# Split weights kept from quarters 1 to 3 for the dilation-4 query projection of quarter 4

## The chip, the core and the metric

The program runs on one core of a Trainium2 chip. Its time is the device time of one execution in microseconds, the median over runs. The engines are PE (matmul; PEld is its weight load), DVE (VectorE), ACT (ScalarE), POOL (GpSimd) and SP, which issues every transfer of this kernel in the order of its own instruction list: a transfer that has to wait holds back all that stand behind it. Sixteen DMA engines carry out what SP issues.

## The reference

A trunk of two layers on 2048 tokens of width 1024, in float32: a gated MLP with a causal spatial mixing inside chunks of 128, then one layer of sliding-window attention with three dilations (1, 4, 16) that share one K/V. The change is in the projection of the second layer:

```python
h = rms_norm(x, norm_g) * (1 + scale) + shift
qz = h @ w_in                      # 1024 -> 3 x 1024 (q of dilations 1, 4, 16) + 1024 (gate z)
q = rms_norm(q, q_norm_g) * (HEAD_DIM ** -0.5)
o, lse = dilated_group_attn(q[:, :, hs], kb, vb, slopes[hs], window, d)   # for each dilation
```

## The kernel before, in words

The 2048 tokens are worked off in four quarters of 512 (`for Q in range(NQ)`); the text counts them 1 to 4, the code 0 to 3. In each quarter `layer_A` does the first layer, then `proj_B` does the projections of the second: blocks 2 and 1 of K/V, `q_block(2)` (dilation 16), `kv_block(0)`, `q_block(1)` (dilation 4), `q_block(0)` (dilation 1) and `z_block`. Local attention of a quarter runs beside the next quarter's first layer. The dilation-16 attention needs all queries of that dilation, so it starts in quarter 4 only, as `wide_attention`, and is dealt out between the matmuls of `kv_block(0)`, `q_block(1)` and `q_block(0)` of that quarter, at a rate set by `rate` and `tick`.

A matmul in full precision is made of three in a faster format: a weight is split into a high part `hi` (a copy in float32r by ACT, line 252) and a low part `lo` (the difference, by DVE, line 253), `split`. `mm3` then does hi x hi, lo x hi and hi x lo. A q or z block (`dense_s`) takes seven products in place of eight, in the manner of Strassen's method: the weights of a product are one quadrant of the matrix ("11", "21", "22") or one of four sums of quadrants made once and stored (t1 to t4, in `wt`). The products run in the order 11, t2, 21, t3, t1, t4, 22. Each takes four k rows; a k row is a tile of 128 x 512, 256 KB as loaded and 512 KB when split, and feeds six matmuls. A product takes 24 of them.

`wunits` brings a k row: SP loads `raw` (pool `rp`, 6 buffers), ACT and DVE split it into `w` (pool `wp`, 8 buffers, so two products). So a raw load waits until the split six k rows earlier has been read, and a split waits until the matmuls eight k rows earlier are through. Every k row is loaded and split again in each of the four quarters.

The dilation-16 attention works on units of one block and four heads. For each unit SP loads the queries `qt` (`ap_`, 2 buffers), DVE copies their scale columns (`rt`, line 1309), PE transposes (`pq`), ACT makes `qT`, PE makes the scores (`ps`, line 1344), DVE adds the bias and finds the maxima (lines 1353 to 1357, into `pr` or `b_s`, then `stat`), ACT takes the exponential (line 1363), PE transposes (`pp`, line 1405), ACT or DVE copies to `pT`, PE multiplies with V (`po`, line 1423), and SP stores the output `ot` to `od`. A `qt` load waits for the transposes of the unit two before it.

The instruction order on each engine is set when the program is built: a scheduler places each instruction by its own estimate of when it can start. An engine then runs its list in that order.

In names of the program, `q31` is quarter 4 (index 3), dilation 4 (group 1); `raw_q31t` and `w_q31t` are a k row of a sum t1 to t4, `raw_q` and `w_q` one of a quadrant. `pd_q31a` and `pd_q31b` are the accumulators of that block.

Of the kernel before, what the change touches and what calls it, by code (L numbers as in the profile page):

```python
# [12 lines left out]
F32 = mybir.dt.float32  # L13
F32R = mybir.dt.float32r
# [4 lines left out]
P = 128  # L19
# [3 lines left out]
NQ = 4  # L23
# [11 lines left out]
def trunk(ctx, tc, out, x, c, a_ada_w, a_ada_b, a_norm_g, a_w_in, a_sgu_g, a_w_spatial,  # L35
          a_b_spatial, a_w_out, kv_ada_w, kv_ada_b, kv_norm_g, w_kv, k_norm_g, b_ada_w,
          b_ada_b, b_norm_g, b_w_in, b_q_norm_g, b_w_out, dbg=None):
    nc = tc.nc
# [26 lines left out]
    gd = dp.tile([2, D], F32, name="gd")  # L65
    wod = dp.tile([2, KT, P, 2, 512], F32, name="wod")
    hd = dp.tile([2, P, KT, 256], F32, name="hd")
    wtd = dp.tile([2, 7, 4, P, 2, 512], F32, name="wtd")
    wt = [[dp.tile([512, 512], F32, name=f"wt{b}_{i}") for i in range(4)] for b in range(6)]

# [184 lines left out]
    def wunits(w, k0, n0, nm, nk=KT, ordered=False):  # L255
        us = []
        for kk in range(nk):
            u = wp.tile([P, 2, 512], F32R, tag="w", name=f"w_{nm}{kk}")
            raw = rp.tile([P, 512], F32, tag="raw", name=f"raw_{nm}{kk}")
            ld = nc.sync.dma_start(raw, w[(k0 + kk) * P:(k0 + kk + 1) * P, n0:n0 + 512])  # L260
            last_ld[0] = ld
            if ordered:
                tc.keep_in_program_order(ld)
            split(u[:, 0, :], u[:, 1, :], raw)
            us.append(u)
        return us

    last_mm, last_ld = [None], [None]
# [274 lines left out]
    def sum_tile(nm):  # L543
        return tp.tile([P, 520], F32, tag="st", name=f"st_{nm}")

    def dense_s(ops, b, nm, evac):


        x, y = ([pst(f"pd_{nm}{c}{i}", "d") for i in range(2)] for c in "ab")
        if flip[0]:  # L550
            x, y = y, x
        flip[0] = not flip[0]
        w, n0 = block_of(b)
        src = {"11": (w, 0, n0), "21": (w, 4, n0), "22": (w, 4, n0 + 512)}
        src.update({f"t{i + 1}": (wt[b][i], 0, 0) for i in range(4)})

        def product(pts, a, w, first):
            us = wunits(*src[w], f"{nm}{w}_", 4)
            store_late(5)
            hh, hl = ops[a]  # L560
            for k in range(4):
                for i in range(2):
                    sl = slice(i * P, (i + 1) * P)
                    mm3(pts[i], hh[:, k, sl], hl[:, k, sl], us[k], first and k == 0, k == 3, True)
                tick(0.2857)
            job = jobs.pop(0) if jobs else None
            if job:
                with tc.issue_after(last_ld[0].ins):
                    job()

        def tmp(n):
            return [sum_tile(f"{nm}{n}{i}") for i in range(2)]

        def add(o, p, q):
            for i in range(2):
                nc.vector.tensor_tensor(o[i][:, 0:512], p[i], q[i][:, 0:512], ALU.add)

        product(x, "11", "11", True)
        u2 = tmp("u")
        for i in range(2):  # L580
            nc.scalar.activation(u2[i][:, 0:512], x[i], AF.Copy)
        product(y, "s2", "t2", True)
        add(u2, y, u2)
        product(x, "12", "21", False)
        for i in range(2):
            evac(i, x[i], 0)
        product(y, "s3", "t3", True)
        u3 = tmp("v")
        add(u3, y, u2)
        product(x, "s1", "t1", True)  # L590
        add(u3, x, u3)
        for i in range(2):
            evac(i + 2, u3[i], 1)
        product(y, "22", "t4", False)
        c21 = tmp("w")
        add(c21, y, u2)
        for i in range(2):
            evac(i + 2, c21[i], 0)
        product(x, "s4", "22", False)
        add(u2, x, u2)  # L600
        for i in range(2):
            evac(i, u2[i], 1)
# [544 lines left out]
    def proj_B(Q, hk, hb, keep, rest, ahead, ready):  # L1147
        def rows(t):
            return slice((Q * TPQ + t) * P, (Q * TPQ + t + 1) * P)

        def kvs(t, g0, n, part):

            return kvd[rows(t), g0:g0 + n // 2, :].rearrange(
                "p g (h two d) -> p g h two d", h=2, two=2)[:, :, :, part, :]

        def ev0(t, pt):
            held = Q == NQ - 1
            kt = head_norm_store(pt, 4, f"k0{Q}_{t}", held)[:, 0:512].rearrange("p (g h d) -> p g h d", g=2, h=2)

            def store():  # L1160
                for g in range(2):
                    nc.sync.dma_start(kvs(t, g, 2, 0)[:, 0], kt[:, g])
            if held:
                stores.append([4, store])
            else:
                store()

        def ev1(t, pt):
            kt = head_norm_store(pt, 2, f"k1{Q}_{t}")
            nc.scalar.activation(kt[:, 256:512], pt[:, 256:512], AF.Copy)  # L1170
            kt = kt.rearrange("p (g h d) -> p g h d", g=2, h=2)
            nc.sync.dma_start(kvs(t, 2, 2, 0)[:, 0], kt[:, 0])
            nc.sync.dma_start(kvs(t, 0, 2, 1)[:, 0], kt[:, 1])

        def ev2(t, pt):
            vt = evt(f"v2{Q}_{t}")
            nc.scalar.activation(vt, pt, AF.Copy)
            vt = vt.rearrange("p (g h d) -> p g h d", g=2, h=2)
            for g in range(2):
                nc.sync.dma_start(kvs(t, 1 + g, 2, 1)[:, 0], vt[:, g])  # L1180

        def kv_block(n, early=None, ready=None):
            dense([hk], w_kv, n * 512, f"kv{Q}{n}", (ev0, ev1, ev2)[n], early, ready)

        def q_block(g):
            def ev(t, src, n):
                if t < 2 and n == 0:
                    c_ = sum_tile(f"qc{g}{Q}{t}")
                    nc.scalar.activation(c_[:, 0:512], src, AF.Copy)
                    src = c_  # L1190
                nm = f"q{g}{n}{Q}_{t}"
                sq = evt(f"hs_{nm}")
                nc.scalar.activation(sq, src[:, 0:512], AF.Square)
                s4 = sp.tile([P, 16], F32, tag="sq", name=f"s4_{nm}")
                nc.vector.tensor_reduce(s4[:, 0:4], sq.rearrange("p (h d) -> p h d", d=P), AX.X, ALU.add)  # L1195
                nc.gpsimd.tensor_scalar(s4[:, 4:8], s4[:, 0:4], 1.0 / P, EPS, ALU.mult, ALU.add)  # L1196
                nc.gpsimd.tensor_tensor(src[:, 516:520], s4[:, 4:8], mhalf[:, 0:4], ALU.pow)
                nc.gpsimd.tensor_tensor(s4[:, 4:8], s4[:, 4:8], src[:, 516:520], ALU.mult)
                nc.gpsimd.tensor_tensor(src[:, 512:516], s4[:, 4:8],
                                        slopes[:, g * 8 + n * 4:g * 8 + n * 4 + 4], ALU.mult)  # L1200
                stores.append([4 if Q == NQ - 1 and g == 2 else 0,
                               lambda: nc.sync.dma_start(qd[g][rows(t), n, :], src)])
            dense_s(hb, g, f"q{Q}{g}", ev)

        def z_block(_):
            def ev(t, src, n):
                held = Q == NQ - 1 and (t, n) not in ((0, 0), (1, 0))
                zt = src[:, 0:512] if held else evt(f"zb{n}{Q}_{t}")
                nc.scalar.activation(zt, src[:, 0:512], AF.Silu)
                put = lambda: nc.sync.dma_start(zd[rows(t), n * 512:(n + 1) * 512], zt)  # L1210
                if Q == NQ - 1:
                    stores.append([-100 if held else 3, put])
                else:
                    put()
            dense_s(hb, 3, f"z{Q}b", ev)

        ops = make_ops(hb, keep, f"b{Q}")
        rate[0] = 1.7
        kv_block(2, {(0, 2): lambda: (rest(), fillers.insert(0, ops))}, ready)
        kv_block(1)  # L1220
        for _ in ops:
            pass
        if ops in fillers:
            fillers.remove(ops)
        while 2 not in combined:
            fill(1)
        q_block(2)
        if Q == NQ - 1:
            fillers.append(wide_attention())
            rate[0] = 9.2  # L1230
        kv_block(0)
        if Q < NQ - 1:
            drain()
            ahead()
        if Q == NQ - 1:
            for n in range(2):
                jobs.extend([None] * 2 + [lambda n=n: load_wo(0, 2 * n), None, None, lambda n=n: load_wo(0, 2 * n + 1), None])
            jobs.extend([None] * 4 + [lambda: (load_wo(1, 0), load_wo(1, 1)), lambda: load_wo(1, 2),
                                      lambda: load_wo(1, 3)])
        q_block(1)  # L1240
        q_block(0)
        if Q == NQ - 1:
            ahead()
        z_block(0)
        store_late(0)

# [436 lines left out]
```

## Time and profile before

| | |
|---|---|
| median of 3 runs | 2929.49 us (2927.91 to 2931.87) |
| the profiled execution | 2928.77 us, of it 2927.1 us span from the first to the last instruction |
| granted TensorE clock | 0.999 |
| `q_block(1)` of quarters 1, 2, 3 | 524 to 562, 1152 to 1190, 1794 to 1832 us |
| `q_block(1)` of quarter 4 | 2448 to 2541 us |

The stretches of the last two rows are read from the starts and ends of the matmuls on `pd_q01` to `pd_q31`. In quarters 1 to 3 the block's 168 matmuls run back to back, in quarter 4 they share PE with the attention, so the block lasts longer. All times in the text count from the start of the span. An engine's idle time matters only where PE has to wait for it.

### The profile page before, as it was taken

How to read it: one execution, taken by the hardware profiler on the slowest of the kernel's cores; microseconds unless marked ns; L12 is line 12 of the kernel's file. 1: busy time of each engine (PE TensorE's matmuls, PEld its weight loads, DVE VectorE, ACT ScalarE, POOL GpSimd, SP SyncE). 2: the span in 40 equal slices, each digit the busy share in tenths (PEclk: the TensorE clock that was granted, in tenths of full speed). 3: DMA queues.
4: the chain of work that ended last, by engine and by line, in shares of the span. 5: the costliest groups of instructions: out<-in, count | busy, mean ns of one | idle time of the engine just before them, and what ended most of it. 6: DMA issues, size and time to landing. Idle time of an engine off the chain costs nothing.

```text
span 2927.1 us, 45613 instructions
## 1 busy us (share of the span) xinstructions
PE 2881.6 (98%) x14608; PEld 2417.7 (83%) x14608; DVE 2161.1 (74%) x4070; ACT 1640.4 (56%) x3378; POOL 718.5 (25%) x1011
## 2 busy tenths in 40 slices
PE   7999999999999999999999999999999999999999
PEld 4788778888888878888888888888888888888887
DVE  6777676687777886887667776877768776878782
ACT  4323345767676355776555365774646367876441
POOL 1047102330000412501233213501414211222312
PEclk9999999999999999999999999999999999999999
DMA  8899976796888976787545976885337967789653
GB/s 280 264 298 341 322 246 191 241 302 213 275 292 307 343 250 213 253 298 245 169 121 191 344 226 213 284 269 168 107 103 250 329 200 240 249 272 336 220 172 112
DMA packets 393812, 713.54 MB, mean 244 GB/s; under 512 B 41722, under 2 KB 141276, under 8 KB 393572
## 3 DMA queue, kind: packets, MB, share of 16 engines
q1 hardware_dynamic: 393572, 710.63, 73.0%
q8 instruction: 116, 1.90, 0.3%
q14 instruction: 124, 1.02, 0.1%
HBM read 552.53 MB, written 157.95 MB: 243 GB/s over the span
## 4 chain that ended last, share of the span: by engine, by line
PE 80%; DMA 9%; DVE 5%; issue 3%; POOL 1%; ACT 1%; SPq 1%; POOLq 0%; ACTq 0%; DVEq 0%
PE pd_kv L281 8%; PE po L1423 4%; PE pd_u L323 3%; PE pd_u L325 3%; PE pd_z L325 3%; PE pd_z L323 3%; PE pd_u L324 3%; PE pd_z L324 3%; PE pd_o L281 2%; PE pm L1011 1%; PE pd_o3a L281 1%; DMA raw_u<-in_a_w_in_dram 1%; PE pd_o1a L281 1%; PE pd_v3b L281 1%; PE pd_v3a L281 1%
## 5 line engine op out<-in xcount | busy, mean ns | idle before, releaser
L281 PE MATMUL pd_kv<-w_kv,hkh 128*128 128x512 f32 x672 | 208.7, 391 | 1.4 <-DVE w_kv L253 1.3
L323 PE MATMUL pd_u<-hAh,w_u 128*128 128x512 f32 x512 | 207.0, 404 | 0.0
L323 PE MATMUL pd_z<-hAh,w_z 128*128 128x512 f32 x512 | 204.1, 399 | 0.0
L325 PE MATMUL pd_u<-hAh,w_u 128*128 128x512 f32 x512 | 200.5, 392 | 0.0
L325 PE MATMUL pd_z<-hAh,w_z 128*128 128x512 f32 x512 | 200.2, 391 | 0.0
L324 PE MATMUL pd_u<-hAl,w_u 128*128 128x512 f32 x512 | 199.7, 390 | 0.0
L324 PE MATMUL pd_z<-hAl,w_z 128*128 128x512 f32 x512 | 199.5, 390 | 0.0
L252 ACT ACTIVATE w_z<-raw_z 128x512 fp32r<-128x512 f32 x128 | 79.9, 631 | 142.0 <-PE pd_z L325 56.6
L252 ACT ACTIVATE w_u<-raw_u 128x512 fp32r<-128x512 f32 x128 | 79.5, 631 | 142.4 <-DMA raw_u<-in_a_w_in_dram 77.2
L1423 PEld LDWEIGHTS po<-kv,pT 128*128 128x128 f32 x1200 | 147.7, 191 | 11.8 <-ACT pT L1269 2.4
L1423 PE MATMUL po<-kv,pT 128*128 128x128 f32 x1200 | 150.8, 275 | 3.2 <-ACT pT L1269 1.6
L281 PEld LDWEIGHTS pd_kv<-w_kv,hkh 128*128 128x128 f32 x672 | 125.4, 188 | 28.5 <-DVE w_kv L253 2.5
L253 DVE TENSOR_TENSOR w_z<-raw_z,w_z 128x512 fp32r<-128x512 f32 x128 | 103.1, 817 | 53.5 <-ACT w_z L252 53.2
L1371 POOL TENSOR_TENSOR dg<-pr,ident 128x256 f32<-128x256 f32 x38 | 30.7, 808 | 434.6 <-DVE stat L1418 226.6
L281 PE MATMUL pd_kv<-w_kv,hkl 128*128 128x512 f32 x336 | 130.7, 390 | 0.0
L1363 ACT ACTIVATE pr<-pr,stat,rt 128x256 f32<-128x256 f32 (+1 forms) x192 | 104.3, 547 | 29.8 <-DVE stat L1357 16.1
L253 DVE TENSOR_TENSOR w_u<-raw_u,w_u 128x512 fp32r<-128x512 f32 x128 | 94.2, 747 | 35.2 <-ACT w_u L252 34.6
L252 ACT ACTIVATE w_q<-raw_q 128x512 fp32r<-128x512 f32 x144 | 89.0, 628 | 49.2 <-PE pd_kv L281 11.5
L253 DVE TENSOR_TENSOR w_q<-raw_q,w_q 128x512 fp32r<-128x512 f32 x144 | 95.8, 688 | 25.0 <-ACT w_q L252 22.8
L1196 POOL TENSOR_SCALAR s_q<-s_q 128x4 f32<-128x4 f32 x96 | 26.9, 280 | 353.7 <-DVE s_q L1195 275.8
L325 PEld LDWEIGHTS pd_u<-hAh,w_u 128*128 128x128 f32 x512 | 96.1, 188 | 21.4 <-DVE w_u L253 0.4
L325 PEld LDWEIGHTS pd_z<-hAh,w_z 128*128 128x128 f32 x512 | 96.1, 188 | 20.7
(906 smaller groups left out, 8511.7 us busy)
## 6 DMA issues: line engine op xcount, KB each, us to landing
raw_q<-in_b_w_in_dram SPq DMA_DIRECT2D x144, 256.0 KB, 3.2
w_o<-wtd SPq DMA_DIRECT2D x72, 512.0 KB, 4.7
raw_u<-in_a_w_in_dram SPq DMA_DIRECT2D x128, 256.0 KB, 4.3
raw_z<-in_a_w_in_dram SPq DMA_DIRECT2D x128, 256.0 KB, 3.7
wtd<-cs SPq DMA_DIRECT2D x56, 512.0 KB, 2.9
qt<-qd SPq DMA_DIRECT2D x96, 260.0 KB, 4.1
raw_v<-in_a_w_in_dram SPq DMA_DIRECT2D x96, 256.0 KB, 4.1
od<-ot SPq DMA_DIRECT2D x96, 256.0 KB, 3.0
```

Source lines behind the costliest of these rows:

```text
L252: nc.scalar.activation(hi, src, AF.Copy)
L253: nc.vector.tensor_tensor(lo, src, hi.bitcast(F32), ALU.subtract)
L281: last_mm[0] = nc.tensor.matmul(pt, a, u[:, w, :], start=f, stop=e, skip_group_check=more)
L323: nc.tensor.matmul(pts[i], wh, hh[:, k, :], start=k == 0, stop=False)
L324: nc.tensor.matmul(pts[i], wh, hl[:, k, :], start=False, stop=False)
L325: nc.tensor.matmul(pts[i], wl, hh[:, k, :], start=False, stop=k == KT - 1)
L1011: nc.tensor.matmul(pm[:, t * P:(t + 1) * P], m[e // 8][:, t, (e % 8) * P:(e % 8 + 1) * P], wst[:, e // 2, :], start=True, stop=True)
L1196: nc.gpsimd.tensor_scalar(s4[:, 4:8], s4[:, 0:4], 1.0 / P, EPS, ALU.mult, ALU.add)
L1363: nc.scalar.activation(pr[:, i, :], pr[:, i, :], AF.Exp, bias=mneg[:, i:i + 1], scale=u["rt"][:, h:h + 1], accum_out=lsum[:, i:i + 1])
L1371: nc.gpsimd.tensor_tensor(dg, prev, ident.unsqueeze(1).broadcast_to([P, hp, P]), ALU.mult)
L1423: nc.tensor.matmul(po[:, h * P:(h + 1) * P], u["pT"][h // hp][:, h % hp, j, :], u["kv"][:, j, kh, 1, :], start=j == 0, stop=j == nk - 1)
```

## The change

A new tensor in HBM, `qsd`, holds split k rows. In quarter 1 each of the seven products of `q_block(1)` stores its split k row 1, in quarter 2 its k row 2, in quarter 3 its k row 3: seven stores of 512 KB in each of three quarters. They are issued in the next product, after its weight loads (`saves`). In quarter 4 the block loads k rows 1, 2 and 3 of every product split, straight into `w` (21 loads of 512 KB in place of 21 of 256 KB), and splits only k row 0. `dense_s` of the other blocks is as before, apart from issuing what is left in `saves`.

```diff
@@ -65,6 +65,7 @@
     gd = dp.tile([2, D], F32, name="gd")
     wod = dp.tile([2, KT, P, 2, 512], F32, name="wod")
     hd = dp.tile([2, P, KT, 256], F32, name="hd")
+    qsd = dp.tile([2, 7, 4, P, 2, 512], F32, name="qsd")
     wtd = dp.tile([2, 7, 4, P, 2, 512], F32, name="wtd")
     wt = [[dp.tile([512, 512], F32, name=f"wt{b}_{i}") for i in range(4)] for b in range(6)]
 
@@ -543,7 +544,9 @@
     def sum_tile(nm):
         return tp.tile([P, 520], F32, tag="st", name=f"st_{nm}")
 
-    def dense_s(ops, b, nm, evac):
+    saves = []
+
+    def dense_s(ops, b, nm, evac, keep=(), kept=()):
 
 
         x, y = ([pst(f"pd_{nm}{c}{i}", "d") for i in range(2)] for c in "ab")
@@ -554,8 +557,22 @@
         src = {"11": (w, 0, n0), "21": (w, 4, n0), "22": (w, 4, n0 + 512)}
         src.update({f"t{i + 1}": (wt[b][i], 0, 0) for i in range(4)})
 
+        place = {"t1": 0, "t2": 1, "t3": 2, "t4": 3, "11": 4, "21": 5, "22": 6}
+
         def product(pts, a, w, first):
-            us = wunits(*src[w], f"{nm}{w}_", 4)
+            us = []
+            for k in range(4):
+                if k in kept:
+                    u = wp.tile([P, 2, 512], F32R, tag="w", name=f"w_{nm}{w}_{k}s")
+                    last_ld[0] = nc.sync.dma_start(u.bitcast(F32), qsd[b, place[w], k])
+                    us.append(u)
+                else:
+                    us += wunits(src[w][0], src[w][1] + k, src[w][2], f"{nm}{w}_{k}", 1)
+            with tc.issue_after(last_ld[0].ins):
+                while saves:
+                    saves.pop(0)()
+            for k in keep:
+                saves.append(lambda u=us[k], k=k: nc.sync.dma_start(qsd[b, place[w], k], u.bitcast(F32)))
             store_late(5)
             hh, hl = ops[a]
             for k in range(4):
@@ -1200,7 +1217,13 @@
                                         slopes[:, g * 8 + n * 4:g * 8 + n * 4 + 4], ALU.mult)
                 stores.append([4 if Q == NQ - 1 and g == 2 else 0,
                                lambda: nc.sync.dma_start(qd[g][rows(t), n, :], src)])
-            dense_s(hb, g, f"q{Q}{g}", ev)
+            split_ks = ((1,), (2,), (3,))
+            if g != 1:
+                dense_s(hb, g, f"q{Q}{g}", ev)
+            elif Q < NQ - 1:
+                dense_s(hb, g, f"q{Q}{g}", ev, keep=split_ks[Q])
+            else:
+                dense_s(hb, g, f"q{Q}{g}", ev, kept=sum(split_ks, ()))
 
         def z_block(_):
             def ev(t, src, n):
@@ -1213,6 +1236,7 @@
                 else:
                     put()
             dense_s(hb, 3, f"z{Q}b", ev)
+            assert not saves
 
         ops = make_ops(hb, keep, f"b{Q}")
         rate[0] = 1.7
```

PE's instruction list keeps its order. The other engines' lists change in the places that follow.

SP, quarter 4, from the end of `q_block(2)` into `q_block(1)` (`kvd` are the stores of K of `kv_block(0)`, `qt_1_1` the queries of the fourth attention unit). Before:

```order
L1289 DMA qt_0_1_23836<-qd_94 128x520
L1162 DMA kvd<-st_hs_k_0_23812 128x2x128
L1289 DMA qt_1_0_23882<-qd_94 128x520
L1162 DMA kvd<-st_hs_k_0_23812 128x2x128
L1162 DMA kvd<-st_hs_k_1_23820 128x2x128 x2
L260 DMA raw_q31t_2_24243<-wt_1_111 128x512
L260 DMA raw_q31t_3_24248<-wt_1_111 128x512
L1289 DMA qt_1_1_23920<-qd_94 128x520
L260 DMA raw_q_0_24390<-in_b_w_in_dram 128x512
```

With the change:

```order
L1313 DMA qt_0_1_23858<-qd_94 128x520
L1313 DMA qt_1_0_23904<-qd_94 128x520
L261 DMA raw_q_00_25071<-in_b_w_in_dram 128x512
L567 DMA w_q_1s<-qsd 128x1024
L567 DMA w_q_2s<-qsd 128x1024
L1313 DMA qt_1_1_23942<-qd_94 128x520
L567 DMA w_q_3s<-qsd 128x1024
L1179 DMA kvd<-st_hs_k_0_23834 128x2x128 x2
L1313 DMA qt_2_0_23989<-qd_94 128x520
```

The first `kvd` stores move behind `qt_1_0` and `qt_1_1`; in front of `qt_1_1` now stand one raw load and the split loads of k rows 1 and 2.

SP, quarter 4, in the middle of `q_block(1)` (`qt_7_1` is attention unit 16 of 32, `st_qc` are finished queries of two token tiles, stored to `qd`). Before:

```order
L1289 DMA qt_7_0_24648<-qd_94 128x520
L1284 DMA kv_8_24778<-kvd 128x512
L260 DMA raw_q_1_25108<-in_b_w_in_dram 128x512
L1433 DMA od_97<-ot_4_1_24615 128x512
L1289 DMA qt_7_1_24695<-qd_94 128x520
L260 DMA raw_q_2_25113<-in_b_w_in_dram 128x512
L1433 DMA od_97<-ot_5_0_24665 128x512
```

With the change:

```order
L1313 DMA qt_7_0_24634<-qd_94 128x520
L1308 DMA kv_8_24755<-kvd 128x512
L1457 DMA od_97<-ot_4_1_24601 128x512
L1219 DMA qd_93<-st_qc_24558 128x520
L1219 DMA qd_93<-st_qc_24568 128x520
L567 DMA w_q31t_1s<-qsd 128x1024
L1313 DMA qt_7_1_24681<-qd_94 128x520
L1457 DMA od_97<-ot_5_0_24651 128x512
L567 DMA w_q31t_2s<-qsd 128x1024
```

The two `qd` stores, which stood 14 rows behind `qt_7_1`, now stand ahead of it, and in place of a raw load a split load.

DVE, quarter 4, at the start of `q_block(1)` (`s_k`, `st_hs_k` are the norm of the last two K tiles, `pT_1_00` the copy of probabilities that the matmul `po` of unit 1_0 reads). Before:

```order
L1356 TENSOR_REDUCE rt_1_1_23969<-b_s 128x4
L1132 TENSOR_REDUCE s_k_2_24037<-st_hs_k_2_24035 128x4
L1357 SCALAR_TENSOR_TENSOR stat_197<-rt_1_1_23969 128x4
L1132 TENSOR_REDUCE s_k_3_24045<-st_hs_k_3_24043 128x4
L1135 TENSOR_TENSOR st_hs_k_2_24035<-pd_kv_2_23828,hr_k_2_24039 128x512
L1135 TENSOR_TENSOR st_hs_k_3_24043<-pd_kv_3_23829,hr_k_3_24047 128x512
L1267 COPY pT_1_00_24102<-pp_1_00_24097 128x512
L1353 SCALAR_TENSOR_TENSOR pr_2_00_24105<-dist,rt_2_0_24026,ps_2_00_24104 128x128 x4
```

With the change:

```order
L1380 TENSOR_REDUCE rt_1_1_23991<-b_s 128x4
L1152 TENSOR_TENSOR st_hs_k_2_24057<-pd_kv_2_23850,hr_k_2_24061 128x512
L1381 SCALAR_TENSOR_TENSOR stat_198<-rt_1_1_23991 128x4
L1149 TENSOR_REDUCE s_k_3_24067<-st_hs_k_3_24065 128x4
L1291 COPY pT_1_00_24115<-pp_1_00_24110 128x512
L1152 TENSOR_TENSOR st_hs_k_3_24065<-pd_kv_3_23851,hr_k_3_24069 128x512
L1377 SCALAR_TENSOR_TENSOR pr_2_00_24118<-dist,rt_2_0_24048,ps_2_00_24117 128x128 x4
L1333 COPY rt_3_0_24195<-qt_3_0_24141 128x8
```

The copy to `pT_1_00` now stands ahead of the normalisation of the last K tile.

## The prediction

> **What bounds the kernel now.** I read the page's busy times first, then the chain that ended last, then busy times by stage, then PE's waits inside the stages that the change touches.
>
> ```profile
> span 2927.1 us, 45613 instructions
> PE 2881.6 (98%) x14608; PEld 2417.7 (83%) x14608; DVE 2161.1 (74%) x4070; ACT 1640.4 (56%) x3378; POOL 718.5 (25%) x1011
> PE 80%; DMA 9%; DVE 5%; issue 3%; POOL 1%; ACT 1%; SPq 1%; POOLq 0%; ACTq 0%; DVEq 0%
> ```
>
> PE is idle for 2927.1 - 2881.6 = 45.5 us in all. No matmul goes, so the change can gain only what PE waits in places that it reaches. The next table gives, for each stretch, its length, then busy time of PE, PEld, DVE, ACT and POOL with counts, granted clock, DMA share and GB/s. The first three rows are `q_block(1)` in quarters 1 to 3; the fourth is the part of quarter 4 in which that block's weights are made and used, the fifth `q_block(0)` after it.
>
> ```profile
> 524.00:562.00 38.00, 38.00 (x170) 31.46 (x169) 26.29 (x42) 26.71 (x54) 11.72 (x23) 1.00 0.78 257
> 1152.00:1190.00 38.00, 38.00 (x169) 31.49 (x168) 26.19 (x42) 26.34 (x53) 11.81 (x23) 1.00 0.78 255
> 1794.00:1832.00 38.00, 38.00 (x170) 31.45 (x169) 26.03 (x42) 26.08 (x53) 11.82 (x23) 1.00 0.78 251
> 2430.00:2541.00 111.00, 106.79 (x732) 95.75 (x731) 89.55 (x236) 91.41 (x262) 16.30 (x32) 1.00 0.75 237
> 2541.00:2613.00 72.00, 69.21 (x438) 60.74 (x436) 54.90 (x134) 55.41 (x152) 11.54 (x26) 1.00 0.79 253
> 2618.00:2665.00 47.00, 46.68 (x223) 38.48 (x222) 35.09 (x75) 30.83 (x68) 10.36 (x9) 1.00 1.02 381
> ```
>
> In quarters 1 to 3 PE never waits, so nothing is to be gained there. In quarter 4 PE waits 111.00 - 106.79 = 4.2 us in the first stretch and 72.00 - 69.21 = 2.8 us in the second: 7.0 us is the ceiling of the gain. DVE (89.55 of 111) and ACT (91.41) are busy for four fifths of the time, so they are full, but they are not the bound. The last row shows that the DMA engines can move 381 GB/s.
>
> PE's waits, first those from 2430 to 2541 (three), then those from 2541 to 2613 (two rows):
>
> ```profile
> PE po L1423 <- ACT pT L1269: 1.6, 1, 1.6
> PE ps L1344 <- DVE stat L1357: 1.5, 1, 1.5
> PE po L1423 <- ACT qT L1316: 0.8, 1, 0.8
> ...
> PE pp L1405 <- DVE b_s L1353: 1.7, 2, 1.0
> PE ps L1344 <- ACT qT L1316: 1.1, 1, 1.1
> ```
>
> **The work taken away.** Quarter 4 loses 21 splits: 21 x 0.628 = 13.2 us of ACT and 21 x 0.688 = 14.4 us of DVE (groups of all `w_q` splits; page).
>
> ```profile
> L252 ACT ACTIVATE w_q<-raw_q 128x512 fp32r<-128x512 f32 x144 | 89.0, 628 | 49.2 <-PE pd_kv L281 11.5
> L253 DVE TENSOR_TENSOR w_q<-raw_q,w_q 128x512 fp32r<-128x512 f32 x144 | 95.8, 688 | 25.0 <-ACT w_q L252 22.8
> ```
>
> This is off the path except where a split stands in front of the attention's own work, so I follow each of the three waits of the first stretch.
>
> The 1.5 us wait, at 2441 us. It goes back to a late `qt`:
>
> ```profile
> 2433.23 2.02 SPq L1162 DMA_DIRECT2D kvd<-st_hs_k  x3
> 2435.30 0.97 SPq L260 DMA_DIRECT2D raw_q31t<-wt  x2
> 2436.37 0.38 SPq L1289 DMA_DIRECT2D qt<-qd  x1
> ...
> 2439.97 0.17 DVE L1309 COPY rt<-qt 128x8 f32<-128x8 f32 x1 [1.70 <-DMA qt<-qd]
> ...
> 2441.20 1.13 PE L1344 MATMUL ps<-kT,qT 128*128 128x128 f32 x8 [1.53 <-DVE stat L1357]
> ```
>
> The change moves the `kvd` stores behind this load, which could bring it up to 3 us forward. But it puts ahead of it a raw load that waits for the split of k row 0, and two split loads, 1 MB, where 0.5 MB of raw loads stood. At 381 GB/s the added 0.5 MB takes 1.4 us. I take 0, and bound it by -1.5 us (the wait goes) and +1.4 us.
>
> The 0.8 us wait, at 2454 us: named is ACT's `qT`, but DVE's copy to `pT`, which `po` reads too, ended at about the same time, behind K's normalisation, which had waited for POOL. With the change that copy stands one normalisation (0.7 us) earlier, and a split that held up ACT is gone. If DVE was last, the wait goes; if PE's own `pq` and the `qT` behind it were, it stays. I take -0.4, between -0.8 and 0.
>
> The 1.6 us wait, at 2505 us. The chain of waits leads to it through SP:
>
> ```profile
> 2488.46 5.26 DMA qt<-qd
> ...
> 2493.82 0.70 DVE w_q31t L253
> 2494.53 0.33 SPq L260
> ...
> 2494.96 0.39 SPq L1433
> ...
> 2495.45 4.05 DMA qt<-qd
> 2499.53 0.17 DVE rt L1309
> 2499.70 1.03 DVE b_s L1353 x4
> 2500.73 0.60 DVE w_q31t L253
> ```
>
> A split on DVE frees a raw buffer, SP's raw load waits for that, and the next `qt` stands behind it on SP. The change removes this knot: split loads wait only for matmuls. But in its place the two `qd` stores of `st_qc` stand ahead of that `qt`, and they wait for POOL:
>
> ```profile
> 2494.64 0.20 POOL L1199 TENSOR_TENSOR st_qc<-s_q,slopes 128x4 f32<-128x4 f32 x1
> ```
>
> From 2494.84, after two stores and a split load (0.3 to 0.4 us of SP each), the `qt` leaves at some 2496.0, 0.5 us later than now. On the other side, DVE drops the 0.6 us split behind `b_s`. I take -0.3, between -1.6 and +0.6.
>
> The 2.8 us of the second stretch lie in `q_block(0)`, which still splits all its rows: 0, with the full 2.8 as the far end.
>
> **The transfers added.** These are the rows for one transfer of each kind (size, median us from issue to landing):
>
> ```profile
> raw_q<-in_b_w_in_dram SPq DMA_DIRECT2D x144, 256.0 KB, 3.2
> w_o<-wtd SPq DMA_DIRECT2D x72, 512.0 KB, 4.7
> raw_u<-in_a_w_in_dram SPq DMA_DIRECT2D x128, 256.0 KB, 4.3
> wtd<-cs SPq DMA_DIRECT2D x56, 512.0 KB, 2.9
> qt<-qd SPq DMA_DIRECT2D x96, 260.0 KB, 4.1
> ```
>
> Quarters 1 to 3: seven stores of 512 KB are 3.67 MB in 38 us, 97 GB/s; 257 + 97 = 354, below the 381 seen. In share of time, 0.78 + 97 / (381 / 1.02) = 1.04, so by the end of the block some 1.5 us of transfers are in arrears. What covers this is the lead of the splits over the matmuls. It is smallest in quarter 3, where DVE ends the first split of the sixth product at 1817.3 and PE needs it at 1821.05:
>
> ```profile
> 1816.59 0.69 DVE L253 TENSOR_TENSOR w_q21t<-raw_q21t,w_q21t 128x512 fp32r<-128x512 f32 x1 [0.77 <-ACT w_q21t L252]
> ...
> 1821.05 5.60 PE L281 MATMUL pd_q21a<-w_q21t,hob 128*128 128x512 f32 x24
> ```
>
> That is 3.8 us, more than 1.5. SP's own part is seven issues of some 0.4 us in 38 us, and in quarter 3 a wait of up to two splits before a store; the raw loads queued behind it are then late by one or two matmul groups (six matmuls each, 24 in 5.44 us, so 1.4 us a group), still within the lead. A store also has to end before its buffer is written again: it starts when its split is done, about seven groups (9.5 us) ahead, and takes 2.9. I cost all of this at nothing; without the cover it would be the 9.7 us a quarter that 7 x 512 KB take at 381 GB/s.
>
> Quarter 4: 21 x 256 KB more are 5.5 MB in 111 us, 50 GB/s: 237 + 50 = 287, share 0.88. Each split load waits for the matmuls eight k rows back, so it lands some seven k rows, over 20 us at this block's pace (28 k rows in 93 us), before its use. PE does not wait for weights. The cost can come only through `qt`, queued behind larger loads: nothing if DVE's freed time takes it up, 6.4 us if not (below). I take 0.
>
> **Sum.** 0 - 0.4 - 0.3 = -0.7 us. The profiled execution took 2928.8 (span plus 1.7 around it), 0.7 below the median of the runs; against that median, 2929.5 - 0.7 = 2928.8. Within 0.2% (5.9 us), which is about what a measurement of this kernel can tell from no change. This case's own range, by the bounds of the terms without the rivals, is 2926 to 2932.
>
> **Rivals.**
>
> *`qt` late in quarter 4 (slower).* 19 units of attention run beside the block, and most of their `qt` loads now stand right behind a 512 KB load. In stages with a DMA share of 0.9 a 256 KB load took 4.3 us (`raw_u`), in the block's own kind 3.2 (`raw_q`): 1.1 us for more load. If each `qt` lands 1.1 us later, DVE, which copies from it in order, loses 19 x 1.1 = 20.9 us and has 14.4 back: 6.5 us reach PE, 2936. For it speaks that DVE already waits for `qt` (1.70 above); against it, that only three of these waits reached PE at all, and that a `qt` has two units between its issue and its use. It decides once a `qt` lands more than 14.4 / 19 = 0.8 us later than now. The Trainium skill (DMA: Bandwidth & Descriptors, section "Bandwidth") puts the ceiling of the engines at 435 GB/s and about 358 for traffic with HBM. This case's 381 lies above the second figure, so the measurement decides against that limit for a single core; by 358 as a limit the 354 GB/s of quarter 1 would just fit, and the share there would be 0.99. The same page (section "Latency and other measured facts") gives HBM access as 0.2 us on average and 2 us at high load; an estimate from it, 1.8 us for each `qt`, would make this rival 19 x 1.8 - 14.4 = 20 us. The rows show 1.1 us, so no run here shows the larger one.
>
> *Stores ahead of the loads in quarters 1 to 3 (slower).* If the engines have none of the 22% free that the share suggests, seven stores put the loads 9.7 us back, 3.8 is covered, and 5.9 us a quarter reach PE: 2929.5 + 17.6 = 2947. Against it: full PE at 381 GB/s.
>
> *All waits from 2430 to 2613 go (faster).* 4.2 + 2.8 = 7.0 us: 2922.5. DVE and ACT have 14 and 13 us more in a stretch where PE lacks 4.2. Against it: each wait above has a second cause that stays.
>
> *Nothing moves*, because what is freed was never waited for: 2929.5, within the forecast's band.
>
> **Chances and range.** Forecast, with the case of nothing moving, 0.55; `qt` late 0.23; stores 0.09; all waits go 0.13. So faster 0.13, same 0.55, slower 0.32. The range reaches from the faster rival, 2922.5, past the first slower one to 2938, and leaves out the stores and little else.
>
> **What would show it.** Right: ACT and DVE lose 21 splits between 2430 and 2541, PE in quarters 1 to 3 stays at 38.00 of 38.00 with a DMA share near 1.0, and PE's waits from 2430 to 2613 sum to 5 to 8 us. Wrong: PE waits for `w_q` or for matmuls' weights in 524 to 562 and its like (stores), DVE waiting for `qt` much longer than now and PE behind `stat` or `pT` for over 10 us (late `qt`), or no PE wait left there (faster). What I can least exclude is a wait that the new order on SP makes between two of the named places.

## The result, and the profile after

| | before | changed |
|---|---|---|
| median of 6 runs | 2929.33 us (2927.91 to 2931.87) | 2939.32 us (2936.96 to 2947.05) |
| ratio to before | | 1.0038 (95% interval 1.0026 to 1.0050) |
| the profiled execution | 2928.77 us, span 2927.1 | 2947.05 us, span 2945.3 |

The change costs 10 us; forecast were 0.7 us less. The profiled execution of the changed kernel is the longest of its six, 7.7 us over their median. The same kernel was therefore profiled once more among the experiments (2938.57 us in the median, span 2939.8), and what is said of it below holds in both profiles, with somewhat other figures, unless one is named. The code has shifted: the splits of lines 252 and 253 are 253 and 254 now, the additions of accumulators (576) 593, the scaling of x (807) 824, the copy from `qt` (1309) 1333, `ps` (1344) 1368 and `stat` (1357) 1381. Line 575 issues the stores, 567 the split loads.

The span and busy times from the page of the changed kernel, then busy times by stage with the columns of the prediction. The first three rows are again `q_block(1)` of quarters 1 to 3, the next two quarter 4.

```profile
span 2945.3 us, 45569 instructions
PE 2888.6 (98%) x14608; PEld 2418.2 (82%) x14608; DVE 2155.5 (73%) x4049; ACT 1627.7 (55%) x3357; POOL 711.6 (24%) x1011
```

```profile
526.00:564.00 38.00, 38.00 (x170) 31.45 (x169) 24.95 (x40) 24.66 (x51) 11.50 (x23) 1.00 0.95 336
1159.00:1197.00 38.00, 38.00 (x170) 31.46 (x169) 25.52 (x40) 24.16 (x50) 11.46 (x23) 1.00 0.94 330
1805.00:1843.00 38.00, 38.00 (x170) 31.46 (x169) 25.58 (x42) 25.62 (x52) 11.75 (x23) 1.00 0.95 334
2446.00:2559.00 113.00, 106.52 (x718) 95.50 (x717) 77.41 (x212) 81.71 (x242) 12.93 (x28) 0.98 0.84 280
2559.00:2630.00 71.00, 68.28 (x432) 60.14 (x431) 55.17 (x134) 55.09 (x151) 12.04 (x26) 1.00 0.79 256
```

In `q_block(1)` of quarters 1 to 3, where the stores are, PE still never waits. In quarter 4 the splits are gone (DVE 89.55 to 77.41 us, ACT 91.41 to 81.71), and PE idles 6.5 + 2.7 = 9.2 us there instead of 4.2 + 2.8 = 7.0 (8.4 in the second profile). So the work went and no time came of it. Where the time went is seen from the lengths of the stages, from the first matmul of one block to that of the next:

| stage, us | before | changed | changed, 2nd profile |
|---|---|---|---|
| up to `q_block(2)` of quarter 1 (nothing changed yet) | 464.3 | 466.1 | 462.1 |
| `q_block(1)` of quarters 1, 2, 3 | 38.1 each | 38.1, 38.1, 38.0 | 38.1 each |
| `q_block(0)` of quarter 1 | 39.0 | 42.5 | 41.8 |
| `q_block(0)` of quarter 2 | 39.0 | 41.7 | 41.1 |
| `q_block(0)` of quarter 3 | 39.4 | 39.5 | 41.8 |
| first layer of quarters 2, 3, 4, sum | 916.2 | 923.3 | 919.9 |
| `q_block(2)` and `kv_block(0)` of quarter 4 | 70.7 | 73.7 | 74.9 |
| `q_block(1)` of quarter 4 | 93.1 | 94.3 | 94.7 |

Two losses are in both profiles and larger than their spread: `q_block(0)` behind the stores, 6.3 and 7.3 us in sum, and the stretch before `q_block(1)` of quarter 4, 3.0 and 4.2. The first layers are longer too, but they are also 3.6 us longer in a kernel without stores and split loads (end of the experiments). PE's waits, in `q_block(0)` of quarter 1 and in that last stretch:

```profile
PE pd_q00b L282 <- DVE st_q00v L593: 1.4, 1, 1.4
PE pd_q00b L282 <- DVE st_q00u L593: 0.6, 1, 0.6
PE pd_q00b L282 <- DVE st_q01u L593: 0.6, 1, 0.6
...
PE ps L1368 <- DVE stat L1381: 3.8, 1, 3.8
```

In the kernel before PE waits for nothing in that block, and the wait for `stat` is 1.5 us. Why, is seen in two places. First ACT around the start of `q_block(0)` of quarter 1, which is at 562.2 us before and at 564.0 after. `x<-x,r_a` is the scaling of the next quarter's input to the first layer, which ACT does here. From the timeline of before, and then the busy times of the first 10 us of the block (ACT is the fourth engine in them):

```profile
554.55 1.71 ACT L252 ACTIVATE w_q<-raw_q 128x512 fp32r<-128x512 f32 x3
...
558.32 5.81 SPq L260 DMA_DIRECT2D raw_q<-in_b_w_in_dram  x2
...
559.63 1.15 ACT L807 ACTIVATE x<-x,r_a 128x1024 f32<-128x1024 f32 x1 [3.37 <-POOL r_a L247]
```

```profile
562.00:572.00 10.00, 10.00 (x46) 8.29 (x45) 8.55 (x15) 10.00 (x17) 8.23 (x14) 1.00 0.66 214
```

The same of the changed kernel:

```profile
562.90 1.15 ACT L824 ACTIVATE x<-x,r_a 128x1024 f32<-128x1024 f32 x1 [2.77 <-POOL r_a L248]
563.96 0.61 ACT L253 ACTIVATE w_q<-raw_q 128x512 fp32r<-128x512 f32 x1
...
565.33 0.33 SPq L261 DMA_DIRECT2D raw_q<-in_b_w_in_dram  x1
...
577.63 0.63 ACT L253 ACTIVATE w_q00t<-raw_q00t 128x512 fp32r<-128x512 f32 x1 [2.20 <-DMA raw_q00t<-wt]
```

```profile
564.00:574.00 10.00, 9.40 (x42) 7.41 (x41) 7.80 (x13) 10.00 (x18) 5.91 (x11) 1.00 0.45 149
```

ACT is busy for all of those 10 us in both kernels: the scalings, the squares of the finished queries and the splits of the new block come together. It reaches the first scaling 2.6 us ahead of the block before and 1.1 us ahead of it after (0.7 in the second profile), and being full it can't make up the 1.5 us.

ACT's list differs here as well, which the places named with the change leave out. Before, three of the four splits of the block's first product stand ahead of the first scaling (the row at 554.55). In the changed kernel two do, and the third stands behind it (563.96), in all three quarters. The load of the third product's first k row waits for just this split to free its raw buffer, so SP issues it 1.3 us after the block's start instead of 3.9 us ahead of it. These 5.2 us come from the new order and from the delay together; the run with small stores below parts the two. Meanwhile the DMA engines, the scarce thing a moment earlier, stand half empty (share 0.45 against 0.66). Then ACT has to wait for the fourth product's loads, which stand behind the third's on SP (2.20 us), DVE's part of the splits follows ACT's, and DVE's additions of the accumulators (`st_q00u`, `st_q00v`) stand in its list behind splits. For these PE waits.

Second, quarter 4. The rows of before are in the prediction (a `qt` issued at 2436.37, copied from at 2439.97, PE back at 2441.20). Of the changed kernel, SP's, DVE's and PE's rows of the timeline, and then busy times in steps of 4 us:

```profile
2447.78 0.36 SPq L567 DMA_DIRECT2D w_q_1s<-qsd  x1
2448.19 0.43 SPq L567 DMA_DIRECT2D w_q_2s<-qsd  x1
2448.73 0.36 SPq L1313 DMA_DIRECT2D qt<-qd  x1
...
2454.54 0.17 DVE L1333 COPY rt<-qt 128x8 f32<-128x8 f32 x1 [4.25 <-DMA qt<-qd]
...
2455.77 2.04 PE L1368 MATMUL ps<-kT,qT 128*128 128x128 f32 x8 [3.75 <-DVE stat L1381]
```

```profile
2452.00:2456.00 4.00, 0.25 (x2) 0.26 (x2) 1.46 (x5) 0.68 (x2) 0.00 (x0) 0.94 1.02 337
2456.00:2460.00 4.00, 4.00 (x18) 3.72 (x19) 2.44 (x8) 2.98 (x11) 0.00 (x0) 0.63 0.78 255
2460.00:2464.00 4.00, 4.00 (x31) 3.69 (x30) 1.53 (x4) 3.58 (x11) 0.19 (x1) 1.00 0.83 286
```

The `qt` takes 5.8 us from its issue to the copy (3.6 before), behind two split loads and a raw one. Counted from the first matmul of `q_block(2)` (2377.5 before, 2390.6 after) it is copied from at 63.9 us instead of 62.5. That is 1.4 us, the upper bound of the prediction (2.0 us in the second profile). What the prediction had no term for comes behind it: after the wait PE runs at a granted clock of 0.63 for 4 us and does 18 matmuls in place of 31, some 1.7 us (estimated from these two counts).

### The profile page after: what moved, and what is told of

Same layout as the page of the kernel before. It is cut to its first block, busy times and chain, and to the rows that moved or that the text cites. A ratio compares the mean times of both kernels' runs of the same rounds, so it can differ in the third digit from the quotient of the medians.

```text
span 2945.3 us, 45569 instructions
## 1 busy us (share of the span) xinstructions
PE 2888.6 (98%) x14608; PEld 2418.2 (82%) x14608; DVE 2155.5 (73%) x4049; ACT 1627.7 (55%) x3357; POOL 711.6 (24%) x1011
## 3 DMA queue, kind: packets, MB, share of 16 engines
q14 instruction: 124, 1.02, 0.1%
## 4 chain that ended last, share of the span: by engine, by line
PE 78%; DMA 9%; DVE 5%; issue 4%; ACT 2%; POOL 1%; SPq 1%; POOLq 0%; DVEq 0%; ACTq 0%
PE pd_kv L282 8%; PE po L1447 4%; PE pd_z L326 4%; PE pd_z L324 4%; PE pd_z L325 4%; PE pd_u L324 4%; PE pd_u L326 4%; PE pd_u L325 3%; PE pd_o L282 2%; PE pd_v L282 2%; PE pm L1028 2%; PE pd_o1a L282 2%; PE pd_o3a L282 1%; PE pd_o2a L282 1%; PE pd_v3b L282 1%
## 5 line engine op out<-in xcount | busy, mean ns | idle before, releaser
L254 DVE TENSOR_TENSOR w_u<-raw_u,w_u 128x512 fp32r<-128x512 f32 x128 | 94.3, 746 | 37.7 <-ACT w_u L253 36.5
L326 PEld LDWEIGHTS pd_u<-hAh,w_u 128*128 128x128 f32 x512 | 96.1, 188 | 21.0
L324 PEld LDWEIGHTS pd_u<-hAh,w_u 128*128 128x128 f32 x512 | 96.4, 188 | 18.7 <-issue 1.7
```

The source lines that it names most:

```text
L254: nc.vector.tensor_tensor(lo, src, hi.bitcast(F32), ALU.subtract)
L324: nc.tensor.matmul(pts[i], wh, hh[:, k, :], start=k == 0, stop=False)
L326: nc.tensor.matmul(pts[i], wl, hh[:, k, :], start=False, stop=k == KT - 1)
```

## The experiments

The kernels of one group ran on one chip, with the kernel before in between. All ratios are to it.

### Stores alone, split loads alone, and small stores

The changed kernel again, with nothing edited:

> The changed kernel again, on the chip and in the rounds of the three others: 2937 to 2940 under each theory. Its trace shows which of the waits recur: theory S wants those of q_block(0) in quarters 1 and 2 again, theory Q the one at the start of q_block(1) of quarter 4.

The stores without the loads:

```diff
-                dense_s(hb, g, f"q{Q}{g}", ev, kept=sum(split_ks, ()))
+                dense_s(hb, g, f"q{Q}{g}", ev)
```

> The 21 stores of quarters 1 to 3 stay; quarter 4 loads its raw rows and splits them as before, so the stored rows are never read. Theory S (the stores are the main loss: the raw loads behind them land later, and the next block, q_block(0), and the next quarter's first layer find their splits late): 2929.3 + 6 to 8 us, 2935 to 2937, with PE waits in q_block(0) of quarters 1 and 2 and at the start of the first layer of quarters 2 to 4. Theory Q (the loss is qt behind the split loads in quarter 4): 2929 to 2931.

The loads without the stores (of other data of the same size, `wtd`, so that q of dilation 4 is not the reference's in quarter 4):

```diff
-                    last_ld[0] = nc.sync.dma_start(u.bitcast(F32), qsd[b, place[w], k])
+                    last_ld[0] = nc.sync.dma_start(u.bitcast(F32), wtd[b, place[w], k])
...
-                dense_s(hb, g, f"q{Q}{g}", ev, keep=split_ks[Q])
+                dense_s(hb, g, f"q{Q}{g}", ev)
```

> No stores in quarters 1 to 3; quarter 4 loads rows 1 to 3 split, taken from the split rows of the first layer's output weights (same size and layout, other values, so q of dilation 4 in quarter 4 is not the reference's). Theory S: close to before, 2929 to 2932, with at most the 3 to 4 us of the wait at the start of q_block(1). Theory Q: as the changed kernel, 2937 to 2940, with PE waits in quarter 4 only.

And the stores alone with 8 of 128 partitions each, 32 KB, which leaves every engine's list as with full stores:

```diff
-                saves.append(lambda u=us[k], k=k: nc.sync.dma_start(qsd[b, place[w], k], u.bitcast(F32)))
+                saves.append(lambda u=us[k], k=k: nc.sync.dma_start(qsd[b, place[w], k, 0:8], u[0:8].bitcast(F32)))
```

> As the kernel with stores alone, but each store moves 8 of 128 partitions (32 KB in place of 512 KB), with the same instruction lists on all engines otherwise. If the bytes of the stores cost the time: 2929 to 2931, as before. If their places cost it (SP waits before a store, and the changed order of splits on ACT and DVE): as with full stores, 2935 to 2937.

| kernel | median, us | ratio (interval) | `q_block(0)` of quarters 1 to 3 over before, sum |
|---|---|---|---|
| before | 2926.73 | | |
| changed, again | 2938.57 | 1.0041 (1.0028 to 1.0053) | +7.3 |
| stores alone | 2942.82 | 1.0049 (1.0037 to 1.0062) | +6.2 |
| loads alone | 2929.61 | 1.0012 (1.0002 to 1.0022) | +0.1 |
| stores of 32 KB | 2932.88 | 1.0016 (1.0006 to 1.0025) | +0.9 |

The loss is the stores' and, within that, mostly their bytes': the same lists with 1/16 of the bytes lose a third as much, and next to nothing in `q_block(0)`. So neither SP's issues and waits for seven more transfers, nor the new order of DVE and ACT that comes with them, is by itself the main cause. The small stores also show what the order does alone. ACT's rows in quarter 1, where `q_block(0)` starts at 557.4:

```profile
549.56 1.14 ACT L253 ACTIVATE w_q<-raw_q 128x512 fp32r<-128x512 f32 x2
554.52 1.15 ACT L824 ACTIVATE x<-x,r_a 128x1024 f32<-128x1024 f32 x1 [3.82 <-POOL r_a L248]
555.57 0.62 ACT L253 ACTIVATE w_q<-raw_q 128x512 fp32r<-128x512 f32 x1
```

The scaling is on time, 2.9 us ahead of the block, but the third split stands behind it. SP issues the third product's first load 0.5, 0.0 and 0.4 us ahead of `q_block(0)` in the three quarters, against 3.9, 3.8 and 3.6 before; with the full stores alone it is 0.8 to 2.1 us after the block's start. So the order uses up most of the lead of these loads at hardly any cost, and the delay by the bytes then falls on PE. That the bytes of all seven stores would cost as much in the old order is not shown: in all runs seven stores come with the new one.

The loads alone gain nothing, though they take the 21 splits away; they lose about 3 us (0.6 to 6.4 by the interval). In their profile the stretch before `q_block(1)` of quarter 4 is 6.4 us longer, with a longer wait for `stat` and half clock around it as above (PE's waits, 2425 to 2450):

```profile
PE ps L1368 <- DVE stat L1381: 4.3, 1, 4.3
PE pq L1337 <- DVE pr L1377: 1.4, 1, 1.4
```

### Which bytes

Four kernels in one group: half of each store, only the early stores, only the late ones, and loads alone with the first product split as before (the last edit is to the kernel with loads alone).

```diff
-                saves.append(lambda u=us[k], k=k: nc.sync.dma_start(qsd[b, place[w], k], u.bitcast(F32)))
+                saves.append(lambda u=us[k], k=k: nc.sync.dma_start(qsd[b, place[w], k, 0:64], u[0:64].bitcast(F32)))
```

> Quarter 4 as before; each of the 21 stores of quarters 1 to 3 writes 64 of its 128 partitions, 256 KB instead of 512 KB. Known: full stores cost 1.0049 of the time before, stores of 32 KB in the same places 1.0016. Theory A (arrears): the loss comes only where the asked-for transfers exceed what the engines move; half stores ask for 0.78 + 0.13 = 0.91 of them, nothing falls behind, so q_block(0) of quarters 1 to 3 is in sum within 1.5 us of before (full stores: +6.2) and the time is 1.001 to 1.002. Theory B (each store pushes the loads behind it by its own length, whatever the share): half of the loss, q_block(0) in sum +3, time 1.003 to 1.0035.

```diff
-            for k in keep:
+            for k in (keep if w in ("11", "t2", "21") else ()):
```

> Quarter 4 as before; in quarters 1 to 3 only the first three products of q_block(1) store their k row (9 stores of 512 KB instead of 21). Theory A: what falls behind is made good in the four products without a store, so q_block(0) loses under 1.5 us in sum, time 1.000 to 1.002. Theory B: 3/7 of the loss, q_block(0) in sum +2.7, time 1.002 to 1.003. Both: q_block(1) stays at 38.1 us.

```diff
-            for k in keep:
+            for k in (keep if w in ("t1", "t4", "22") else ()):
```

> Quarter 4 as before; in quarters 1 to 3 only the last three products of q_block(1) store their k row (9 stores of 512 KB, the last of them at the start of q_block(0)). Theory A: the same bytes as in the run with early stores, but the raw loads of q_block(0) stand right behind them, so most of the loss of full stores stays: q_block(0) in sum +4 to +6, time 1.003 to 1.005. Theory B: as with early stores, +2.7 in sum, time 1.002 to 1.003.

```diff
-                if k in kept:
+                if k in kept and w != "11":
```

> No stores; quarter 4 loads k rows 1 to 3 of six products split (from the tensor of other split weights, so that dilation 4 of quarter 4 is computed with wrong weights of the same size), and splits the first product's four k rows as before. On SP the rows in front of the second dilation-16 block's second query load are then those of before. Theory H: the wait of 4.3 us for stat before q_block(1) of quarter 4 comes from the raw load and the two split loads in front of that query load; it returns to 1.5 us, the stretch from the first matmul of q_block(2) to that of q_block(1) goes from 77.1 us to 70 to 72, the clock there stays at 1.00, and the time is 0.9985 to 1.000 of before. Rival: the wait comes from the new order of DVE and ACT there; the stretch stays at 74 or more and the time at 1.001 as with all loads.

| kernel | median, us | ratio (interval) | `q_block(0)` over before, quarters 1, 2, 3 |
|---|---|---|---|
| before | 2927.04 | | |
| half of each store | 2940.05 | 1.0037 (1.0024 to 1.0050) | +0.5, +0.7, +2.3 |
| early stores | 2934.06 | 1.0020 (1.0011 to 1.0029) | +0.8, 0.0, +1.1 |
| late stores | 2929.88 | 1.0015 (1.0007 to 1.0024) | 0.0, 0.0, 0.0 |
| loads, first product split | 2928.55 | 1.0000 (0.9991 to 1.0008) | +0.1, +0.1, 0.0 |

Theory A (nothing is lost while the share of the whole block stays below 1) falls with the half stores: share 0.89, and still +3.5 us. The late stores, which were to hurt, and the early ones, which were to be made good, came out the other way round; but the last late store of quarter 1 was issued 10.8 us ahead of `q_block(0)`, not at its start as had been assumed. Theory B (each store costs its length) fits the half stores and the early ones, and fails at the late ones, which carry as many bytes as the early ones and cost `q_block(0)` nothing. Early and late stores can be compared: both kernels keep the order of before on ACT, three splits ahead of the first scaling. The seven stores and their halves have the new order, so part of what lies between them and these two is the order's. What both had overlooked is in the halves of the block. Busy times of the first 20 us of `q_block(1)` of quarter 1 and of the rest, of before:

```profile
524.10:544.10 20.00, 20.00 (x90) 16.58 (x89) 13.92 (x22) 14.37 (x30) 4.28 (x7) 1.00 0.90 302
544.10:562.20 18.10, 18.10 (x82) 14.99 (x81) 12.36 (x20) 12.45 (x25) 7.46 (x18) 1.00 0.64 203
```

With the early stores, and then with the late ones:

```profile
519.20:539.20 20.00, 20.00 (x89) 16.55 (x89) 12.62 (x20) 12.34 (x24) 2.40 (x4) 1.00 1.02 359
539.20:557.20 18.00, 18.00 (x81) 14.92 (x80) 13.02 (x22) 12.18 (x28) 9.58 (x19) 1.00 0.71 231
```

```profile
524.70:544.70 20.00, 20.00 (x90) 16.58 (x89) 13.91 (x22) 14.34 (x30) 4.29 (x7) 1.00 0.93 321
544.70:562.80 18.10, 18.10 (x82) 14.99 (x81) 12.04 (x20) 12.07 (x24) 7.96 (x17) 1.00 0.75 263
```

The share of 0.78 is a mean of 0.90 and 0.64. The first half is nearly full before the change, since the outputs of `q_block(2)` and of `kv_block(0)` are stored in it; with the early stores it is full (1.02), and ACT does 24 instructions in it where it did 30. With the late stores it keeps its 30. So the arrears arise in the first 20 us, and by the end of the block ACT's squares of x, POOL's `r_a` and ACT's scaling are late. How late is read from the row that the result showed: ACT reaches its first scaling 2.6, 2.5 and 2.3 us ahead of `q_block(0)` before, 0.7 and 1.8 us ahead and just at its start with the early stores, and 2.1, 2.9 and 2.6 us ahead with the late ones. The quarters with the largest delay have the largest loss. The changed kernel bears this out in quarter 3 of its first profile: ACT comes 2.3 us ahead there, as before, and `q_block(0)` loses 0.1 us.

The last of the four settles quarter 4: with the list of before in front of that `qt` the wait in front of `ps` falls to 1.3 us, the clock stays at 1.00, the stretch before `q_block(1)` is 71.9 us instead of 77.1, and the time is that of before. Also settled is that 18 splits less are worth nothing there that could be told (interval 0.9991 to 1.0008).

### Whether ACT is what carries the delay

If the 1.5 us matter only because ACT is full, they should stop mattering when it isn't. In quarters 2 to 4 the scaling of x was cut to 64 of 1024 columns, which takes some 3 us from the full stretch. This was done with all the stores (quarter 4 as before) and without any.

```diff
-            nc.scalar.activation(xts[t], xts[t], AF.Copy, scale=r[:, t:t + 1])
+            nc.scalar.activation(xts[t][:, 0:64], xts[t][:, 0:64], AF.Copy, scale=r[:, t:t + 1])
```

> Quarter 4 as before, all 21 stores of 512 KB; besides, ACT's scaling of the next quarter's x (four instructions of 128 x 1024, 1.05 us each, in the 12 us in which ACT is never idle around the start of q_block(0) of quarters 1 to 3) is done for 64 of the 1024 columns only, so that the first layer of quarters 2 to 4 works on x that is mostly unscaled. Theory C: the stores make the raw loads, and with them the chain of ACT's squares, POOL's r_a and ACT's scaling, 1 to 2 us late; the loss comes because ACT, full for 12 us from there on, can't make that up. With some 3 us of that work gone it can: q_block(0) of quarters 1 to 3 is in sum under 2 us longer than in the kernel without stores and with the same cut (full stores without the cut: +6.2). Theory D: the loss comes from the late raw loads alone, whatever ACT has to do; the sum stays at +5 to +6.

> The kernel before with the same cut in ACT's scaling of x (64 of 1024 columns in quarters 2 to 4), as the control. Both theories: q_block(0) of quarters 1 to 3 stays at 39.0, 39.0 and 39.4 us, since PE waits for nothing there, and the time is within 0.1% of before.

And a version of the change from what was left of it, the late products alone, stored and loaded (9 stores, 9 split loads):

```diff
-                if k in kept:
+                if k in kept and w in ("t1", "t4", "22"):
...
-            for k in keep:
+            for k in (keep if w in ("t1", "t4", "22") else ()):
```

> The change cut down to what the runs so far leave standing: only the last three products of q_block(1) (t1, t4, 22) store their k rows in quarters 1 to 3 and are loaded split in quarter 4, so 9 stores and 9 split loads. Nothing of the computation is left out. Q_block(0) of quarters 1 to 3 as before (39.0 to 39.4), the wait for stat before q_block(1) of quarter 4 at 1.5 to 2 us with a clock of 1.00. If the loads gain nothing (the run that split the first product as before: 1.0000), the time is 1.000 to 1.0015; if the freed 9 splits are worth something in quarter 4, 0.999.

| kernel | median, us | ratio (interval) | `q_block(0)` of quarters 1 to 3, us |
|---|---|---|---|
| before | 2925.48 | | 39.0, 39.0, 39.4 |
| cut, with all stores | 2929.64 | 1.0015 (1.0006 to 1.0023) | 39.2, 39.1, 41.1 |
| cut, without stores | 2927.70 | 1.0005 (0.9995 to 1.0014) | 39.1, 39.1, 39.4 |
| late version | 2927.96 | 1.0002 (0.9992 to 1.0012) | 39.0, 39.1, 39.4 |

With ACT relieved the stores cost 1.9 us by the medians in place of 14 to 16, and `q_block(0)` loses 1.8 us in place of 6.2, as theory C asked. But part of this loss has only moved: `q_block(1)` is now 1.2 and 0.9 us longer in quarters 1 and 2, where the order has changed once more and two more splits than before, the last of them behind the scaling, stand ahead of an addition that PE needs,

```profile
PE pd_q00a L282 <- DVE st_q01w L593: 1.1, 1, 1.1
```

and quarter 3, with the order of the stores alone, still loses 1.7 of its 2.6. The two blocks together lose some 4 us in place of 6.2. So the loss as a whole nearly goes when ACT has less to do, but that a full ACT carries the delay into `q_block(0)` is shown in part only, since the cut changed the order too. Where the rest of the loss went is not settled.

The late version costs nothing and gains nothing that could be told. None of the kernels beats the one before.

Not settled is what remains in the kernels with small or with late stores, 0.15%. Their first layers are 5.7 and 2.8 us longer in sum than in the profile of before, but the cut kernel without a store is 3.6 longer too, so single profiles don't show how much of that is the stores'. The same goes for the 7.1 and 3.7 us of the changed kernel. PE's wait at the start of quarter 2's first layer, for `m` from ACT, is 0.7 us before, 2.5 and 0.5 in the two profiles of the changed kernel, and 2.6 in the cut kernel without a store.

## Why the prediction was wrong

**The transfers in quarters 1 to 3 (costed at nothing).** This is the step that failed. It read the room from the mean share of the whole block and took the arrears of 1.5 us for covered by the lead of the splits. The runs show 6.3 and 7.3 us lost in `q_block(0)` instead. Three things in it:
- The arrears came out right in size (1.5 us, by ACT's first scaling) by luck: the block's mean hides a first half at 0.90, and in that half full engines moved 355 to 359 GB/s with the stores, not the 381 of the stretch that the top speed was read from. For the first half that gives 302 GB/s x 20 us = 6.0 MB asked for before, plus 3 or 4 stores of 0.52 MB, 7.6 to 8.1 MB, of which 7.1 fit; 0.5 to 1.0 MB late are 1.4 to 2.8 us.
- The cover was real where it was read. PE waits for nothing in `q_block(1)`, as forecast (38.00 of 38.00, share 0.94 to 0.95 for "near 1.0").
- But a lead that is used up has to be earned back, and the prediction didn't ask where. The row that answers it, ACT's 10.00 of 10.00 us in the next stretch, is in the profile of before. There the delay, with the third split now behind the scaling, became 2.1 to 3.5 a quarter in five of the six quarters of the two profiles (0.1 in the sixth).

The rival "stores ahead of the loads in quarters 1 to 3" came nearest to the cause, with 0.09. Its sign, PE waiting for weights in `q_block(1)`, did not show, and its 5.9 us a quarter, taken at the same wrong place, were too many: measured are 6.3 to 7.3 us in all three.

**The 1.5 us wait in quarter 4 (0, between -1.5 and +1.4).** The lateness of `qt` was at the bound, +1.4 us; the half clock behind the wait, 1.7 us, was missing. Together they make up the 3.0 us by which the stretch is longer (in the second profile 2.0 and 2.2 us, for 4.2).

**The 0.8 us and the 1.6 us wait (-0.4 and -0.3).** Without the wait for `stat`, PE's waits from the hand-over to the end of the block sum to 2.7 us before (4.2 - 1.5) and to 2.7 after (6.5 - 3.8; 3.4 in the second profile). The two were replaced by others of the same sum; the rival that all waits go fell with them. The 2.8 us of `q_block(0)` stayed, as taken.

**`qt` late in quarter 4 (rival, 0.23).** One late `qt` reached PE, not 19. DVE's waits for `qt` did grow in the stretch, from 10.8 us (9 waits) to 20.2 (14), but in the kernel with the first product split as before they are 19.1 and the time is that of before: DVE had that much time to spare. The waits of PE, which were to sum to 5 to 8 us if the forecast was right, gave 9.2, by the hand-over alone. The 1.1 us of this rival rested on a reading that was off: 4.3 us is the median of `raw_u` over all four quarters, and in the stage with a share of 0.92 (120 to 233 us) these loads took 6.1.

**The work taken away.** The 21 splits left the stretch (35 before, 14 after) with 12.9 us of ACT and 14.2 of DVE, near the forecast 13.2 and 14.4, and PE got nothing of them, as the forecast had it.

Two figures of the prediction are 0.1 us off, and nothing hangs on them: 7 x 512 KB at 381 GB/s take 9.6 us, and the 6.4 us of a late `qt` are 6.5 by its own sum.

## What to carry to other kernels

Read the room for added transfers in stretches no longer than the lead that is to cover them, and put the transfers where there is room: of the stores alone, seven a quarter cost 0.49%, the first three 0.20%, and the last three, in the emptier half, 0.15% and nothing in the block behind them. A delay that PE doesn't feel where it arises is not yet free: follow it to the first stretch behind it in which an engine that works in order is full, and look whether the added instructions have changed that engine's list there. And work taken off an engine that is not the bound is worth only the waits that it ends; here that was none.

## What was not expected of the hardware

Around a wait PE may drop to half clock (granted 0.50) for a while. In three profiles the drop came about when PE took up work again, and lasted 3.4 us: behind the 3.8 us wait of the changed kernel, behind one of 1.4 us with the small stores, and behind one of 1.28 us in the late version. In two it came inside the wait and lasted 6.8 us: in the second profile of the changed kernel 1.5 us after PE had stopped (wait 3.8 us), in the kernel with the loads alone after 1.3 us (wait 4.3 us). In the kernel with the first product split it didn't come behind a wait of 1.28 us, so the length of the wait doesn't decide alone. First two slices of 1 us from the second profile, both inside the wait (granted clock third from the end):

```profile
2448.00:2449.00 1.00, 0.00 (x0) 0.00 (x0) 0.00 (x0) 0.64 (x2) 0.00 (x0) 1.00 0.98 370
2450.00:2451.00 1.00, 0.00 (x0) 0.00 (x0) 0.48 (x2) 0.00 (x0) 0.00 (x0) 0.50 0.96 328
```

Then the late version (the wait in its first row, the clock in the second):

```profile
2433.00:2437.00 4.00, 2.45 (x10) 1.15 (x8) 2.75 (x11) 3.51 (x11) 0.00 (x0) 1.00 0.85 310
2437.00:2441.00 4.00, 3.82 (x16) 3.60 (x17) 2.94 (x9) 3.72 (x12) 0.00 (x0) 0.57 0.40 132
```

and of the kernel with the first product split:

```profile
2432.00:2436.00 4.00, 2.31 (x9) 1.07 (x7) 2.75 (x11) 3.64 (x12) 0.00 (x0) 1.00 0.82 301
2436.00:2440.00 4.00, 3.95 (x29) 3.69 (x30) 3.07 (x10) 3.64 (x13) 0.00 (x0) 1.00 0.59 154
```

The same eight matmuls of `ps` behind the wait took 2.03 us in the one and 1.16 in the other. The Trainium skill (TensorE: Matmul & The Clock Gate, section "Part 1: The HAM clock gate") gives half rate after an idle window of about 3.4 us. The slow stretches of 3.4 and 6.8 us are one and two such lengths. But in four of the five the clock fell when PE had stood still for only 1.3 to 1.5 us, so a standstill of that length is not needed, as far as these traces show.
